# A deeper ring of early weight loads and later context loads in a three-block float32 transformer kernel

## Chip, cores and metric

The kernel runs on one core of one Trainium2 chip. The metric is the device time of one execution in microseconds. The notes below use the engines' short names: PE is TensorE (matrix products), PEld its weight loads, DVE is VectorE, ACT is ScalarE, POOL is GpSimd, and SP is the SyncE queue that issues the DMAs.

## The reference, cut to what matters

The program is a chain of three blocks on 512 tokens of width 2048, all in float32. Only the head of the first block lies near the change:

```python
sh_x, sc_x, gt_x = split(silu(c)     @ w_ada + b_ada, 3)   # w_ada: 2048 x 6144
sh_c, sc_c, gt_c = split(silu(c_ctx) @ w_ada + b_ada, 3)
h_x = rms_norm(x,   norm_g) * (1 + sc_x) + sh_x            # 512 x 2048
h_c = rms_norm(ctx, norm_g) * (1 + sc_c) + sh_c            # 256 x 2048
px = split_cols(h_x @ w_in)
pc = split_cols(h_c @ w_in)
oa, ob, oc, od = four attention mixers on px and pc
x  = x + gt_x * (concat(oa, ob, oc, od) @ w_out)
...
```

Mixer a lets every query see the 256 context keys and the 512 tokens; its first key projection is the first use of `h_c`. Two more blocks follow (a pooled block with sparse attention, and a block of sliding-window attention).

## The kernel before, in words

Every product of float32 operands is made of three matmuls on split halves: hi·hi, lo·hi and hi·lo. A weight therefore passes through three hands after its DMA: ACT writes `hi` (L569), POOL or DVE subtracts to get `lo` (L579), PE multiplies (L506 to L508 for the tokens, 512 columns wide; L511 to L513 for the context, 256 wide).

`Net.stream()` (L519) brings the weights in. They come as units of 128x512 float32 (256 KB), two units a pair, in one fixed order. The first 152 units are the start of the program: 128 units of `w_ada` and, woven between them, 24 units of the first six projections (two query heads into `px`, gates into `pc`, two halves of `S` and `O`). The modulation has four column blocks b; each is 16 units for the scale and 16 for the shift, four of them per step of PE (L682, 16 matmuls that use the raw weights as they are). After each half block PE turns the result (L656) and DVE writes `modv`. When both halves of block b stand, four k-slices of `h_x` can be made for it (`make_h`, L775): a product with the row of inverse norms (L787, DVE or POOL), the affine step and the split on ACT (L801, L303), and the low half (L306). The projections of block b run with them; the six of the last block stand at the end of the stretch. Behind them comes the first key projection of mixer a ("the first key tile" below): for each of the 16 k three matmuls on `hx` (L506 to L508) and three on `hc` (L511 to L513).

The pairs land in a ring of buffers. `ring(i)` (L530) names the pool of a pair: `wr`, `pt`, or one buffer each of two of `P`. A pair goes out as one DMA of 512 KB where its two units are neighbours in memory and in the buffer, else as two of 256 KB. SP issues in order, and a pair's DMA waits until the buffers of its pool are free; `used()` (L572) frees them when both units are done. Each DMA also waits for the one eight places ahead of it.

The context takes the same way as the tokens: `inputs()` (L719) loads it in four DMAs of 512 KB (L732, tile `xt`, source `cT`), ACT squares the 16 slices (L744), DVE or POOL adds them, PE sums over the partitions (L406), and `row()` (L383) makes the row `rc` (PE L395, ACT L398). `CMARK` (L26) says behind which pair each of the four loads may go: (40, 6) is pairs 40, 46, 52 and 58. From `rc` follow the 16 products (L787 on `xt` and `rc`), the affine steps and the splits into `hc`.

No engine's order is written by hand. A list scheduler (`Sched`, L70) runs the program's coroutines against modelled costs while the kernel is built; each operation goes to the engine's queue in the order in which the model starts it, and for `lo`, `b` and `h` it also picks DVE or POOL. So a shift of one load can give other orders on every engine behind it.

Of the kernel before, what the change touches and what calls it, by code (L numbers as in the profile page):

```python
# [16 lines left out]
DRAM = bass.MemoryType.DRAM  # L17

KT = 16
EARLY = 160  # L20
LAG = (12, 4)
WAYS = 3
EARLY_OUT = ["px", "px", "pc"]
D_ORDER = "r0 q0 h0 q1 g0 h1 g1 r1 g2 q2 h2 g3 q3 - h3"
XMARK = (4, 0.4)
CMARK = (40, 6)  # L26
EPS = 1e-6
NEG = -1e30
LOG2 = math.log(2)
# [12 lines left out]
def f32(ap):  # L42
    return ap.bitcast(F32)
# [150 lines left out]
def D2(n=0, k=1, ptr=0):  # L194

    return ("DVE", Port(D(n, k=k, ptr=ptr)[1]))
# [7 lines left out]
def A(n=0, ptr=0, acc=0, k=1):  # L204
    return ("ACT", k * (0.19 + n * 0.833e-3 + 0.093 * (ptr + acc)))


def G(n=0, k=1, bias=0.0):

    return ("POOL", Port(k * (0.15 + n * 2.2e-3)), bias)  # L210
# [13 lines left out]
class Net:  # L224
# [294 lines left out]
    def stream(self):  # L519

        ready = [Ev() for _ in self.units]
        raws = [Ev() for _ in range((len(self.units) + 1) // 2)]
        left = [min(2, len(self.units) - i) for i in range(0, len(self.units), 2)]
        nc = self.nc

        def whole(i):

            return len(self.units[i]) > 2

        def ring(i):  # L530

            return (["wr"], ["pt"], ["P", "P"], ["wr"], ["pt"], ["P", "P"])[i // 2 % 6] if i < EARLY else ["wr"]

        def wring(i):
            return ("w", "act")[i % 2] if i < EARLY else "w"

        def loads():
            for i in range(0, len(self.units), 2):
                n = min(2, len(self.units) - i)
                tags = ring(i)  # L540
                raw = yield from self.alloc(tags[0], name="wr")
                raw = [raw[:, :512], raw[:, 512:]] if len(tags) == 1 else [raw[:, :512]]
                if len(tags) > 1:
                    raw.append((yield from self.alloc(tags[1], name="wr"))[:, :512])
                src = [self.units[i + j][0] for j in range(n)]
                if n == 2 and len(tags) == 1 and src[1].offset == src[0].offset + 512:
                    both = bass.AP(tensor=raw[0].tensor, offset=raw[0].offset, ap=[raw[0].ap[0], [1, 1024]])
                    x = src[0]
                    src = [bass.AP(tensor=x.tensor, offset=x.offset, ap=[x.ap[0], [1, 1024]])]
                    dst = [both]  # L550
                else:
                    dst = raw
                for x, y in zip(dst, src):
                    yield ("SP", 0.06)
                    nc.sync.dma_start(x, y)
                self.dma_free = max(self.dma_free, self.s.now) + 1.46
                self.s.set_at(raws[i // 2], self.dma_free + 1.9, raw)
                self.s.set(self.marks.setdefault(i // 2, Ev()))

        def hi():  # L560
            for i in range(len(self.units)):
                yield raws[i // 2]
                r = raws[i // 2].val[i % 2]
                if whole(i):
                    self.s.set(ready[i], r)
                    continue
                w = yield from self.alloc(wring(i), (2, 512), F32R, "w")
                yield A(512)
                nc.scalar.activation(w[:, 0], r, AF.Copy)  # L569
                self.spawn(lo(i, w, r), 1)  # L570

        def used(i):  # L572
            left[i // 2] -= 1
            if left[i // 2] == 0:
                self.free(*ring(i))

        def lo(i, w, r):
            e = yield [D2(512), G(512, bias=WSLACK)]
            (nc.gpsimd if e == "POOL" else nc.vector).tensor_tensor(w[:, 1], r, f32(w[:, 0]), op=OP.subtract)  # L579
            used(i)  # L580
            self.s.set(ready[i], w)

        def main():
            for i, (_, fn, *_) in enumerate(self.units):
                if fn is None:
                    continue
                if whole(i):
                    for j in range(i, i + 4):
                        yield ready[j]
                    yield from fn([ready[j].val for j in range(i, i + 4)])  # L590
                    for j in range(i, i + 4):
                        used(j)
                    continue
                yield ready[i]
                w = ready[i].val
                yield from fn(w[:, 0], w[:, 1])
                self.free(wring(i))
        self.spawn(loads(), 0)
        self.spawn(hi(), 1)
        self.spawn(main(), 9)  # L600
# [633 lines left out]
    def block1(self):  # L1234
# [55 lines left out]
        def ctx():  # L1290
            rc = (yield from self.alloc("b", name="rc"))[:, :256]
            cs, cfin = self.inputs(a["cT"], 256, rc, 4, *CMARK)
            self.make_h(cs, cfin, 256, rc, 1, mods, hc, 4)
# [1098 lines left out]
```

## Time and profile before

| | |
|---|---|
| median of three runs | 2716.51 us (2716.38 to 2718.41) |
| the profiled execution | 2720.7 us, of which the span of its instructions is 2718.9 us |
| mean granted TensorE clock | 0.988 |
| busy share of the span | PE 98%, DVE 50%, ACT 44%, POOL 41% |
| chain that ended last | PE 93%, DVE 2%, DMA 2% |
| DMA | 315.97 MB, mean 116 GB/s; 355 and 328 GB/s in the first two of 40 slices of the span |

A slice is 68 us. The page's first part gives each engine's busy time; the second shows the span in 40 slices with the granted clock in tenths; the windows show the same for any stretch; the timeline lists instructions with their start, their duration and, in brackets, how long the engine stood idle before one and what released it. Start times are from the start of the span.

### The profile page before, as it was taken

Reading aid. Unit: us, or ns where it says so; the run is one execution under the profiler, and the core shown is the slowest. Engines: PE = TensorE matmul, PEld = TensorE weight load, DVE = VectorE, ACT = ScalarE, POOL = GpSimd, SP = SyncE. Lnnn points to the kernel's source line nnn. Section 1 sums busy time; section 2 is a strip of 40 time slices with the busy share of each in tenths; the row PEclk is TensorE's granted clock in tenths of the full one; section 3 lists DMA queues with packets and bytes.
Section 4 is the critical chain, followed back from the end, with each engine's and each line's share of the span. In section 5 each row is a group of like instructions: output and inputs, shape, how many; then the busy total and the mean of one; then the engine's idle time right before and its main releaser. Section 6 shows DMA issues by size and latency. Waiting matters only on the chain.

```text
span 2718.9 us, 36544 instructions
## 1 busy us (share of the span) xinstructions
PE 2655.8 (98%) x13324; PEld 2192.5 (81%) x13324; DVE 1362.8 (50%) x3151; ACT 1194.6 (44%) x2415; POOL 1121.8 (41%) x923
## 2 busy tenths in 40 slices
PE   7989999999999999899999999999999999999999
PEld 3568888888888887688887888887888888888787
DVE  3456763335552655422359466664225777676300
ACT  3444443333342445433442455554334656566421
POOL 1352333334333334344445554653444333344544
PEclk8989999999999999999999999999999999999999
DMA  9936542222221223244223322224442222222343
GB/s 355 328 102 213 182 159 69 72 72 78 70 70 64 69 67 116 78 146 145 86 78 101 109 90 89 96 87 144 147 144 90 90 93 98 84 88 86 128 142 125
DMA packets 121959, 315.97 MB, mean 116 GB/s; under 512 B 13874, under 2 KB 23986, under 8 KB 121780
## 3 DMA queue, kind: packets, MB, share of 16 engines
q1 hardware_dynamic: 121780, 313.65, 34.8%
q8 instruction: 104, 1.70, 0.3%
q14 instruction: 75, 0.61, 0.1%
HBM read 293.02 MB, written 32.11 MB: 120 GB/s over the span
## 4 chain that ended last, share of the span: by engine, by line
PE 93%; DVE 2%; DMA 2%; ACT 1%; POOL 0%; issue 0%; SPq 0%; ACTq 0%; DVEq 0%; POOLq 0%
PE px L506 23%; PE px L507 23%; PE px L508 23%; PE T L413 4%; PE S L1128 2%; PE pc L511 2%; PE pc L513 1%; PE pc L512 1%; PE T L427 1%; DMA wr<-w 1%; PE S L1825 1%; PE T L682 1%; PE S L1824 1%; PE O L1103 1%; PE O L1104 1%; PE O L1102 1%
## 5 line engine op out<-in xcount | busy, mean ns | idle before, releaser
L579 POOL TENSOR_TENSOR w<-wr,w 128x512 fp32r<-128x512 f32 x699 | 913.5, 1307 | 1418.6 <-ACT w L569 1390.2
L569 ACT ACTIVATE w<-wr 128x512 fp32r<-128x512 f32 x736 | 463.8, 631 | 1007.2 <-PE px L508 648.5
L506 PE MATMUL px<-u,w 128*128 128x512 f32 x1248 | 495.8, 397 | 0.0
L507 PE MATMUL px<-u,w 128*128 128x512 f32 x1248 | 488.3, 391 | 0.0
L508 PE MATMUL px<-u,w 128*128 128x512 f32 x1248 | 487.7, 391 | 0.0
L506 PE MATMUL px<-hx,w 128*128 128x512 f32 x816 | 330.1, 405 | 6.5 <-ACT w L569 3.5
L507 PE MATMUL px<-hx,w 128*128 128x512 f32 x816 | 323.2, 396 | 5.5 <-DVE hx L306 5.5
L508 PE MATMUL px<-hx,w 128*128 128x512 f32 x816 | 322.0, 395 | 1.8 <-POOL w L579 1.8
L506 PE MATMUL px<-o,w 128*128 128x512 f32 x752 | 297.3, 395 | 8.2 <-ACT o L303 8.2
L507 PE MATMUL px<-o,w 128*128 128x512 f32 x752 | 297.3, 395 | 3.6 <-POOL o L306 2.4
L508 PE MATMUL px<-o,w 128*128 128x512 f32 x752 | 295.9, 394 | 0.0
L508 PEld LDWEIGHTS px<-u,w 128*128 128x128 f32 x1248 | 234.7, 188 | 51.0
L506 PEld LDWEIGHTS px<-u,w 128*128 128x128 f32 x1248 | 235.4, 189 | 41.9
L507 PEld LDWEIGHTS px<-u,w 128*128 128x128 f32 x1248 | 235.3, 189 | 41.0
L306 DVE TENSOR_TENSOR pt<-T,pt 128x512 fp32r<-128x512 f32 (+2 forms) x208 | 127.7, 616 | 162.7 <-ACT pt L303 161.9
L508 PEld LDWEIGHTS px<-hx,w 128*128 128x128 f32 x816 | 154.7, 190 | 38.1 <-POOL w L579 3.2
L506 PEld LDWEIGHTS px<-hx,w 128*128 128x128 f32 x816 | 155.4, 190 | 31.3 <-ACT w L569 6.2
L507 PEld LDWEIGHTS px<-hx,w 128*128 128x128 f32 x816 | 155.3, 190 | 25.4 <-DVE hx L306 7.6
L506 PEld LDWEIGHTS px<-o,w 128*128 128x128 f32 x752 | 142.9, 190 | 39.1 <-ACT o L303 10.0
L507 PEld LDWEIGHTS px<-o,w 128*128 128x128 f32 x752 | 143.1, 190 | 37.7 <-POOL o L306 5.2
L508 PEld LDWEIGHTS px<-o,w 128*128 128x128 f32 x752 | 143.0, 190 | 29.7
L303 ACT ACTIVATE pt<-T 128x512 fp32r<-128x512 f32 (+2 forms) x208 | 110.1, 537 | 123.8 <-PE O L1104 57.3
(339 smaller groups left out, 4219.0 us busy)
## 6 DMA issues: line engine op xcount, KB each, us to landing
wr<-w SPq DMA_DIRECT2D x237, 512.0 KB, 3.5
wr<-wout SPq DMA_DIRECT2D x89, 512.0 KB, 4.1
wr<-wada SPq DMA_DIRECT2D x37, 512.0 KB, 6.5
gw<-wada SPq DMA_DIRECT2D x64, 256.0 KB, 5.7
wr<-w SPq DMA_DIRECT2D x58, 256.0 KB, 3.7
wr<-wada SPq DMA_DIRECT2D x54, 256.0 KB, 6.2
x<-xr SPq DMA_DIRECT2D x32, 256.0 KB, 4.3
xr<-x SPq DMA_DIRECT2D x32, 256.0 KB, 4.6
```

The costliest lines, as they stand in the source:

```text
L303: nc.scalar.activation(hi, src, AF.Copy)
L306: eng.tensor_tensor(lo, src, f32(hi), op=OP.subtract)
L413: self.nc.tensor.transpose(p[:, j * 128:(j + 1) * 128], x, self.ident)
L427: nc.tensor.matmul(p[:, j * gq:(j + 1) * gq], sq[:, j * 128:(j + 1) * 128], self.ones[:, 0:1] if gq == 1 else self.halves, start=True, sto ...
L506: mm(px, hi[:, s], x[0], **kw)
L507: mm(px, hi[:, s], x[1], start=False, stop=False)
L508: mm(px, lo[:, s], x[0], **ke)
L511: mm(pc, lo[:, s], c[0], **kw)
L512: mm(pc, hi[:, s], c[0], start=False, stop=False)
L569: nc.scalar.activation(w[:, 0], r, AF.Copy)
L579: (nc.gpsimd if e == "POOL" else nc.vector).tensor_tensor(w[:, 1], r, f32(w[:, 0]), op=OP.subtract)
L1128: self.nc.tensor.matmul(o, l, r, start=i == 0, stop=i == len(ops) - 1)
```

## The change

It edits two constants and the two functions that name a unit's buffers.

```diff
-EARLY = 160
+EARLY = 140, 160
...
-CMARK = (40, 6)
+CMARK = (66, 3)
...
         def ring(i):
 
-            return (["wr"], ["pt"], ["P", "P"], ["wr"], ["pt"], ["P", "P"])[i // 2 % 6] if i < EARLY else ["wr"]
+            if i < EARLY[0]:
+                return (["wr"], ["pt"], ["P", "P"], ["p", "p"], ["wr"], ["pt"], ["P", "P"])[i // 2 % 7]
+            return (["wr"], ["pt"], ["P", "P"])[i // 2 % 3] if i < EARLY[1] else ["wr"]
 
         def wring(i):
-            return ("w", "act")[i % 2] if i < EARLY else "w"
+            return ("w", "act")[i % 2] if i < EARLY[1] else "w"
```

For the first 140 units the ring is seven pairs deep instead of six: a pair in two buffers of the pool `p` comes in, which nothing else uses that early. The four context loads go behind pairs 66, 69, 72 and 75 instead of 40, 46, 52 and 58; pair 75 is the last one of the start. Lines above L531 keep their numbers; those below stand two further down. Since a pair in `P` or `p` is two buffers, the loads of `w_ada` change from 37 of 512 KB and 54 of 256 KB to 32 and 64.

The orders differ over the first 350 us or so. Three places matter here. In all of them the number behind a name tells one buffer's use from another's.

On PE, before: the row `rc` of the context is summed (T_977) in the middle of the third projection of block b = 2.

```order
L506 MATMUL pc_438<-hx_848,w_891 128x512
L507 MATMUL pc_438<-hx_848,w_891 128x512
L508 MATMUL pc_438<-hx_848,w_891 128x512
L395 MATMUL T_977<-b_961,ones 128x128 x2
L506 MATMUL pc_438<-hx_851,w_891 128x512
L507 MATMUL pc_438<-hx_851,w_891 128x512
```

On PE, now: the same sum (T_1257) stands in the last projection of block b = 3, six matmuls ahead of the first key tile (px_1283, pc_1284), whose fourth matmul reads `hc`.

```order
L508 MATMUL O_531<-hx_1098,w_1073 128x512
L395 MATMUL T_1257<-b_1208,ones 128x128 x2
L506 MATMUL O_531<-hx_1101,w_1073 128x512
L507 MATMUL O_531<-hx_1101,w_1073 128x512
L508 MATMUL O_531<-hx_1101,w_1073 128x512
L506 MATMUL O_531<-hx_1104,w_1073 128x512
L507 MATMUL O_531<-hx_1104,w_1073 128x512
L508 MATMUL O_531<-hx_1104,w_1073 128x512
L506 MATMUL px_1283<-hx_335,w_1135 128x512
L507 MATMUL px_1283<-hx_335,w_1135 128x512
L508 MATMUL px_1283<-hx_335,w_1135 128x512
L511 MATMUL pc_1284<-hc_1289,w_1135 128x256
```

So the row has moved from one projection section to the next, and nothing of `hc` can be made ahead of it.

On ACT, before: `rc` is copied out and seven slices of `hc` are done ahead of the last four slices of `hx`. These are the first rows of that stretch, and the two with which the last `hx` begins.

```order
L398 ACTIVATE rc_92<-T_977 128x256
L801 ACTIVATE b_994<-b_994,modv 128x256
L303 ACTIVATE hc_1008<-b_994 128x256
...
L801 ACTIVATE b_1149<-b_1149,modv 128x512
L303 ACTIVATE hx_1157<-b_1149 128x512
```

On ACT, now: three squares of the fourth context load (xt_1003) stand right ahead of those last slices of `hx` (the affine steps b_1087 to b_1090).

```order
L571 ACTIVATE w_1068<-wr_1000 128x512
L571 ACTIVATE w_1073<-wr_1000 128x512
L746 ACTIVATE b_1029<-xt_1003 128x256
L746 ACTIVATE b_1032<-xt_1003 128x256
L746 ACTIVATE b_1093<-xt_1003 128x256
L803 ACTIVATE b_1087<-b_1087,modv 128x512
L303 ACTIVATE hx_1095<-b_1087 128x512
```

The copy of `rc` and all 16 slices of `hc` have gone behind them, to the place after the last gate's `th`.

On POOL, now: behind the two halves w_1254 and w_1262 begin the 16 products and 16 low halves of `hc`, all on POOL (32 rows, with three L581 between them). Before, 14 of the 16 products were on DVE, and the low halves were spread from the row `rc` on.

```order
L581 TENSOR_TENSOR w_1254<-wr_1045,w_1254 128x512
L581 TENSOR_TENSOR w_1262<-wr_1045,w_1262 128x512
L789 TENSOR_TENSOR b_1278<-xt_841,rc_92 128x256
L789 TENSOR_TENSOR b_1279<-xt_841,rc_92 128x256
L306 TENSOR_TENSOR hc_1289<-b_1278,hc_1289 128x256
L306 TENSOR_TENSOR hc_1289<-b_1279,hc_1289 128x256
L789 TENSOR_TENSOR b_1299<-xt_841,rc_92 128x256
```

Products and low halves now share one queue with the weights' low halves.

## Rows read from the trace of the kernel before

**Rows 1.** The page: the span, and its first part's line on PE.

```profile
span 2718.9 us, 36544 instructions
...
PE 2655.8 (98%) x13324; PEld 2192.5 (81%) x13324; DVE 1362.8 (50%) x3151; ACT 1194.6 (44%) x2415; POOL 1121.8 (41%) x923
```

**Rows 2.** Windows of 10 us: stretch, length, busy time per engine, clock, DMA share, GB/s.

```profile
90.00:100.00 10.00, 10.00 (x53) 5.47 (x52) 1.28 (x9) 1.26 (x2) 2.57 (x2) 1.00 0.79 263
...
150.00:160.00 10.00, 8.62 (x24) 5.90 (x24) 5.83 (x9) 5.83 (x13) 7.36 (x8) 0.60 0.01 2
...
180.00:190.00 10.00, 10.00 (x55) 7.79 (x54) 6.86 (x17) 1.75 (x4) 4.26 (x5) 1.00 0.18 45
```

**Rows 3.** Timeline of PE, 70 to 140 us: start, duration, instruction, idle before.

```profile
71.03 0.95 PE L656 MATMUL T<-sel,b 128*128 128x2 f32 x8
...
79.08 0.50 PE L506 MATMUL px<-hx,w 128*128 128x512 f32 x1 [1.65 <-ACT w L569]
...
85.00 1.73 PE L682 MATMUL T<-wr,cst 128*32 128x512 f32 x8
...
113.88 0.50 PE L506 MATMUL px<-hx,w 128*128 128x512 f32 x1 [1.53 <-ACT w L569]
...
139.15 0.95 PE L656 MATMUL T<-sel,b 128*128 128x2 f32 x8
```

**Rows 4.** DMA issues: size of one, median us from issue to landing.

```profile
xt<-cT SPq DMA_DIRECT2D x4, 512.0 KB, 8.0
```

**Rows 5.** Timeline of SP, 104 to 109 us.

```profile
105.32 0.53 SPq L732 DMA_DIRECT2D xt<-cT  x1
```

**Rows 6.** Windows of 2 us around the first projections of b = 1 and b = 2.

```profile
80.00:82.00 2.00, 1.56 (x4) 1.29 (x5) 1.27 (x2) 1.14 (x4) 0.39 (x1) 0.50 1.03 395
112.00:114.00 2.00, 0.47 (x2) 0.12 (x2) 0.69 (x1) 1.55 (x4) 0.04 (x1) 1.00 1.01 370
```

**Rows 7.** Timeline of DVE, 71 to 76 us.

```profile
72.54 2.49 DVE L787 TENSOR_TENSOR b<-xt,rx 128x512 f32<-128x512 f32 x4
```

**Rows 8.** Timeline of DVE, 136 to 160 us.

```profile
140.66 6.73 DVE L787 TENSOR_TENSOR b<-xt,rx 128x512 f32<-128x512 f32 x4
```

**Rows 9.** Timeline of POOL, 126 to 170 us.

```profile
138.05 8.78 POOL L579 TENSOR_TENSOR w<-wr,w 128x512 fp32r<-128x512 f32 x6
...
163.15 1.30 POOL L579 TENSOR_TENSOR w<-wr,w 128x512 fp32r<-128x512 f32 x1 [1.29 <-issue]
```

**Rows 10.** Timeline of PE, 140 to 193 us.

```profile
143.92 0.50 PE L506 MATMUL px<-hx,w 128*128 128x512 f32 x1 [3.01 <-ACT hx L303]
148.57 0.79 PE L507 MATMUL px<-hx,w 128*128 128x512 f32 x1 [4.14 <-DVE hx L306]
...
154.53 0.80 PE L507 MATMUL px<-hx,w 128*128 128x512 f32 x1 [1.22 <-DVE hx L306]
...
158.10 0.40 PE L506 MATMUL px<-hx,w 128*128 128x512 f32 x1
...
173.84 0.39 PE L506 MATMUL px<-hx,w 128*128 128x512 f32 x1
...
175.92 0.40 PE L506 MATMUL px<-hx,w 128*128 128x512 f32 x1
...
191.88 1.04 PE L1661 MATMUL T<-b,b 33*32 33x512 f32 x2
```

**Rows 11.** Timeline of ACT, 108 to 170 us.

```profile
126.66 0.38 ACT L398 ACTIVATE rc<-T 128x256 f32<-128x256 f32 x1 [1.84 <-PE T L395]
127.54 0.60 ACT L801 ACTIVATE b<-b,modv 128x256 f32<-128x256 f32 x1 [0.49 <-DVE b L787]
128.17 0.42 ACT L303 ACTIVATE hc<-b 128x256 fp32r<-128x256 f32 x1
```

**Rows 12.** The tile `hc`, 100 to 200 us: times are min/median/max in ns, then first and last start.

```profile
L306 POOL TENSOR_TENSOR hc<-b,hc x16: 726/738/1175, 128.7 to 169.1; 128x256 fp32r<-128x256 f32 x16
```

**Rows 13.** Line 787, 120 to 170 us, in the same form.

```profile
L787 POOL TENSOR_TENSOR b<-xt,rc x2: 742/822/902, 152.2 to 165.1; 128x256 f32<-128x256 f32 x2
```

## Prediction

> **What bounds the kernel now.** I read the page first [rows 1]: PE is busy for 2655.8 of 2718.9 us. The reader should see that only some 63 us of the span are left to win, so the next question is where they lie. The windows answer it [rows 2]: from 180 us on PE is busy in all of its 10 us, while at 150 to 160 us it runs at a granted clock of 0.60 and DMA stands still. From 180 us on the program is a fixed queue of PE work, and the orders behind the first 350 us are the same before and after. So the end of the kernel moves by as much as PE's place in that queue moves, and I measure everything at one point: the end of the first key tile and of the two small matmul pairs of L1661 around it. Before, that is 191.88 + 1.04 = 192.9 us [rows 10].
>
> The timeline of PE tells what bounds the start [rows 3]. Up to 139.15 us, the last L656, PE works through the modulation as fast as `w_ada` arrives, with projection sections between in which it does not wait for DMA (263 GB/s at 90 to 100 us, [rows 2], against 395 where it does wait, [rows 6]). Behind 139.15 us the `hx` of the last block are made, PE idles up to 154.53 us, runs at half clock until 158.10, and reaches the first key tile at 173.84 [rows 10].
>
> **The change, part by part.**
>
> *The context loads leave the middle.* Four loads of 512 KB are 4 x 0.524 MB; at 395 GB/s each takes 1.33 us of the DMA [rows 4, 6]. All four stood ahead of most of the last `w_ada` loads (the last issue at 105.32 us, [rows 5]). Now the first two go between the last pairs of `w_ada`, in the stretch of the third block's projections, where DMA has slack (the 263 against 395 GB/s above), and the others behind all `w_ada`. I count three loads as gained for the last L656, since the fourth was already in such slack: 3 x 1.33 = 4.0 us.
>
> *Two more units in the ring.* While PE is in a projection section the ring fills and DMA slackens. One more pair, 0.524 MB, is 1.33 us more of loads done there. There are three such sections (b = 0, 1, 2), so this is worth between 0 and 4.0 us. I take 2.2, nearer to the middle: the start of b = 1 (79.08 to 85.00 us, [rows 3]) is also bound by its `hx` and its weight halves, which more loads don't bring. That pairs are now split into two DMAs more often costs no PE time; the queue's rate is the same for a mix of both sizes in the rows here. Together the last L656 moves by 6.2, from 139.15 to about 133.0 us. Ends: 4.0 and 8.0, and 3 if the ring gives nothing and PE's own work eats part of the rest.
>
> *The last block's `hx`.* Before, DVE began their products at 140.66 us and took 6.73 for four, 1.68 each, beside six weight halves on POOL [rows 8, 9]; alone they take 0.62 each [rows 7]. Now three squares of the fourth context load stand on ACT ahead of the affine steps. Its DMA goes out last of a burst that waits for PE to read pair 68, some 6 us ahead of the last L656, so at about 127 us; it lands 8.0 later [rows 4], at 135. That is no later than DVE's first product can be through (134.0 for `modv`, then 0.62), so it costs 0 to 1.5 us; I take 0.8. The weight halves on POOL are mostly done by then, so of the (1.68 - 0.62) x 4 = 4.2 us I take back 3.0. The last `hx` comes 6.2 - 0.8 + 3.0 = 8.4 us earlier. PE's half clock behind that pause lasts as long as before (148.57 to 158.10, [rows 10]), since the pause is much the same. The first key tile starts at 173.84 - 8.4 = 165.4 us.
>
> *What is given back: the context itself.* Before, `rc` stood at 126.66 + 0.38 = 127.0 us [rows 11] and the last low half of `hc` began at 169.1 [rows 12], ahead of the tile that reads it. Now the sum over partitions stands six matmuls ahead of the tile. Six matmuls at 0.23 are 1.4, so it runs at about 164.0, and `rc` is out at 164.5. Behind `rc` POOL has 32 passes in one queue. The nearest rows are 0.738 for a low half [rows 12] and 0.742 for a product [rows 13], both on 128x256: 32 x 0.74 = 23.7 us. Three weight halves stand between them, 3 x 1.30 = 3.9 us by the single one in POOL's rows [rows 9]. The first low half waits for one affine step and one split on ACT, 0.60 + 0.42 [rows 11], of which a second product hides most: 0.4. For passes that DVE disturbs (0.902 at most in the row of products, [rows 13]) I add 0.6. The last `hc` stands at 164.5 + 23.7 + 3.9 + 0.4 + 0.6 = 193.1, and its three matmuls end 0.5 later, at 193.6.
>
> PE alone needs (175.92 - 173.84) / 2 = 1.04 us per k [rows 10]; `hc` comes every two passes, 1.48, or 1.72 with the halves between. So PE, which has no other order than px, pc, px, pc, waits at each k, and all that it had won it spends here. Nothing covers this: the next rows of PE all stand behind the tile. Both pairs of L1661, of which one stood inside the tile before, now come behind it, since the program starts those tables only when the last `hc` stands: 193.6 + 2 x 1.04 = 195.7 us.
>
> *The sum.* 195.7 - 192.9 = +2.8 us. Against the profiled execution that gives 2720.7 + 2.8 = 2723.5; the median of the runs stands 4.2 below it (2716.5), so the forecast is **2719.3 us**. Note that a better or worse start cancels only in part: if the tile starts 1 us earlier, `rc` does too, and the end with it. With the passes at their shortest, 0.726 [rows 12], 0.4 us are won; with all of them at 0.90, 32 x 0.16 = 5.1 more are lost, so 2724.4. With a start gain of 8.0 instead of 6.2 it is 2717.5; with 4.0, 2721.5.
>
> A rule on the passes: the Trainium skill's page "SBUF — State Buffer", section "Who interferes with whom", says that a DVE instruction with two SBUF inputs and a GpSimd instruction that reads SBUF share a port pair as an exclusive lock, and the one that comes later waits. The trace agrees: four products of 0.62 alone took 1.68 each beside POOL's weight halves [rows 7 to 9]. By that rule the 32 passes lie nearer to the 0.90 end wherever DVE still runs the rope and gate steps, and the sum would be up to 2724.4; I keep the short price because DVE has given the products of `hc` away and so has less to collide with.
>
> **The rivals.**
>
> *Slower, by the clock.* In the tile PE now waits up to 0.7 us at every k. If the granted clock falls to 0.5 there, a k costs twice its 1.04, 2.08 us, more than the 1.72 at which `hc` comes, and PE is the bound: 165.4 + 16 x 2.08 = 198.7 instead of 193.6. Up to 5.1 more, 2724.4; half of it, with recovery inside the tile, gives 2721.9; the full one with a half clock of some 9 us behind it (as at 148.57 to 158.10, [rows 10]), which loses half of that on top, 2729. I price it at 2724.4. For it: at 80 to 82 us the clock was 0.50 after PE had waited for loads and halves; against it: at 112 to 114 us PE was busy for 0.47 of 2 us and stayed at 1.00 [rows 6]. It decides if the waits come at every k as they do here. The Trainium skill's page "TensorE: Matmul & The Clock Gate", section "HAM oscillation — how this bites in real kernels", describes that: a kernel whose PE waits inside each tile falls back to the slow clock in every tile. Chance 0.17.
>
> *Slower, by the loads.* The start gains only 3 us: the eight DMAs in flight, not the buffers, limit the run-ahead, and more halves than full pairs fill those eight places. Then all moves 3.2 later: 2722.5. For it: more DMAs of 256 KB are issued. Against it: three context loads are gone from the middle in any case. Chance 0.16.
>
> *Faster.* `hc` does not bind: the tile starts at 165.4 and runs through at 1.04 per k, and the kernel wins the 8.4 us, 2708.1. It would need two passes of POOL in 1.04 us, or products that go out ahead of the low halves and ACT. Against it: 0.726 is the shortest pass in the rows [rows 12]. A half-way case (the start wins 10 us or more and the tile loses less) gives 2710. Chance 0.12.
>
> **How the numbers follow.** The forecast has 0.55, the two slower rivals 0.33, the faster one 0.12. This kernel's measurement can tell about 0.2%, 5.4 us, from no change: faster is below 2711.1, slower above 2721.9. The forecast case reaches from 2715 to 2724 by its bounds (start gain, pass time); I give 0.50 of it to no change and 0.05 to slower. The slower rivals are both priced above the line. So: faster 0.12, same 0.50, slower 0.38. For 8 in 10 I leave out the faster rival's lower half and the clock's worst case: 2711.5 to 2727.0.
>
> **What the new profile would show.** Right: the last L656 at 131 to 135 us; the first matmul of the first key tile at 164 to 167; `rc` (now L398 behind the last `th`) at about 164.5; 32 passes on POOL from there to about 193, with PE's L512 waiting for POOL's `hc` at most k; L1661 twice behind the tile; 1.00 in the clock at 165 to 195. The first rival shows as a clock of 0.5 there, the second as a last L656 at 136 or later. The forecast is wrong if PE's idle time inside the tile sums to less than 5 us, or if the queue of PE behind 200 us shows waits that the old one did not have.

## Result and profile after

The change made the kernel slower: 2733.72 us (median of four runs, 2731.72 to 2735.34) against 2716.95 us (four runs, 2716.38 to 2718.41). The ratio is 1.0054, 95% interval 1.0039 to 1.0068. The forecast was 2719.3 us in a range of 2711.5 to 2727.0; the time lies above it. The profiled executions stand 2733.04 to 2720.7 us, 12.3 apart; the one of before lay 3.75 us above the median of its runs, the one of after 0.7 below. All medians leave out the only execution in a slow state, 8738.10 us in the run e8.

The page of the changed kernel, against [rows 1]: the span has grown by 12.0 us, and PE's busy time has not.

```profile
span 2730.9 us, 36536 instructions
## 1 busy us (share of the span) xinstructions
PE 2654.2 (97%) x13324; PEld 2194.2 (80%) x13324; DVE 1349.9 (49%) x3130; ACT 1199.5 (44%) x2422; POOL 1126.9 (41%) x937
```

So PE stands idle for 76.7 us instead of 63.1. The windows of 10 us say where, against [rows 2], whose row for 180 to 190 us had PE busy for all of it.

```profile
140.00:150.00 10.00, 3.82 (x16) 2.59 (x16) 6.18 (x13) 6.17 (x11) 6.50 (x6) 0.82 0.94 341
...
170.00:180.00 10.00, 8.27 (x36) 6.12 (x34) 3.21 (x7) 6.26 (x14) 8.30 (x11) 0.85 0.16 52
180.00:190.00 10.00, 7.08 (x31) 5.70 (x32) 0.00 (x0) 5.45 (x13) 10.00 (x14) 0.84 0.00 0
190.00:200.00 10.00, 8.77 (x46) 7.13 (x46) 3.55 (x2) 7.52 (x16) 10.00 (x14) 0.96 0.10 28
```

From 180 to 200 us POOL is busy without a gap and PE is not: the first key tile waits for the context, as forecast. But the tile should have begun at 165.4 us. The timeline of PE, against [rows 3, 10], shows when things came.

```profile
25.17 1.92 PE L684 MATMUL T<-wr,cst 128*32 128x512 f32 x4 [10.93 <-DMA wr<-wada]
...
32.71 1.87 PE L658 MATMUL T<-sel,b 128*128 128x2 f32 x8
...
84.96 0.51 PE L506 MATMUL px<-hx,w 128*128 128x512 f32 x1 [1.82 <-ACT hx L303]
86.34 0.50 PE L507 MATMUL px<-hx,w 128*128 128x512 f32 x1 [0.88 <-DVE hx L306]
...
140.28 0.95 PE L658 MATMUL T<-sel,b 128*128 128x2 f32 x8
148.12 0.79 PE L506 MATMUL px<-hx,w 128*128 128x512 f32 x1 [6.07 <-ACT hx L303]
...
173.29 0.39 PE L506 MATMUL px<-hx,w 128*128 128x512 f32 x1
...
199.52 0.39 PE L513 MATMUL pc<-hc,w 128*128 128x256 f32 x1 [1.17 <-POOL hc L306]
...
200.67 0.28 PE L513 MATMUL pc<-hc,w 128*128 128x256 f32 x1
```

The last L658 (L656 before) comes at 140.28 instead of 139.15 us, where 133.0 was forecast; the tile begins at 173.29 instead of 173.84; and it ends at 200.67 + 0.28 = 200.95 us instead of 191.95. It held one pair of L1661 before and holds none now, so PE stands 9.0 + 1.04 = 10.0 us further back. Of the other 2 us, 1.4 are small waits behind it: in the five stretches of 25 us from 200 to 325 us PE lacks 0.94, 0.68, 0, 0.33 and 0 us, where it lacked 0.28, 0, 0, 0 and 0.30 before.

Three other timelines of the changed kernel belong to this. SP, where the fourth context load goes out, and ACT, where the context's squares and `rc` stand (against [rows 11]):

```profile
137.34 0.37 SPq L734 DMA_DIRECT2D xt<-cT  x1
```

```profile
143.93 1.03 ACT L746 ACTIVATE b<-xt 128x256 f32<-128x256 f32 x3 [0.70 <-DMA xt<-cT]
146.59 0.81 ACT L803 ACTIVATE b<-b,modv 128x512 f32<-128x512 f32 x1 [1.62 <-DVE b L789]
...
172.11 0.39 ACT L398 ACTIVATE rc<-T 128x256 f32<-128x256 f32 x1
```

And DVE, against [rows 8], with the add of those squares ahead of the products for `hx`:

```profile
141.26 0.60 DVE L664 TENSOR_SCALAR modv<-T,vec 128x2 f32<-128x2 f32 x4 [2.26 <-PE T L658]
144.38 0.50 DVE L751 TENSOR_TENSOR b<-b,b 128x256 f32<-128x256 f32 x1 [2.52 <-ACT b L746]
144.80 3.55 DVE L789 TENSOR_TENSOR b<-xt,rx 128x512 f32<-128x512 f32 x4
```

The passes for `hc` in the view of tiles and lines, against [rows 12, 13]: 32 on POOL, at 0.73 each.

```profile
L306 POOL TENSOR_TENSOR hc<-b,hc x16: 717/729/744, 175.4 to 199.4; 128x256 fp32r<-128x256 f32 x16
...
L789 POOL TENSOR_TENSOR b<-xt,rc x16: 718/732/747, 173.5 to 196.8; 128x256 f32<-128x256 f32 x16
```

### The profile page after: what moved, and what is told of

Read it like the earlier page. It is cut to its first block, busy times and chain, and to the rows that moved or that the text cites. A ratio compares the mean times of both kernels' runs of the same rounds, so it can differ in the third digit from the quotient of the medians.

```text
span 2730.9 us, 36536 instructions
## 1 busy us (share of the span) xinstructions
PE 2654.2 (97%) x13324; PEld 2194.2 (80%) x13324; DVE 1349.9 (49%) x3130; ACT 1199.5 (44%) x2422; POOL 1126.9 (41%) x937
## 4 chain that ended last, share of the span: by engine, by line
PE 91%; DVE 2%; DMA 2%; POOL 1%; ACT 1%; issue 1%; SPq 0%; DVEq 0%; ACTq 0%; POOLq 0%
PE px L506 23%; PE px L507 23%; PE px L508 23%; PE T L413 4%; PE S L1130 2%; PE pc L511 1%; PE pc L513 1%; PE pc L512 1%; PE T L427 1%; PE T L684 1%; PE S L1827 1%; PE S L1826 1%; PE O L1105 1%; PE O L1106 1%; PE O L1104 1%
## 5 line engine op out<-in xcount | busy, mean ns | idle before, releaser
L581 POOL TENSOR_TENSOR w<-wr,w 128x512 fp32r<-128x512 f32 x700 | 912.5, 1304 | 1463.2 <-ACT w L571 1444.3
```

## The experiments

Four theories came out of this; the first two began as one, called Q in the first expectations (the context's queue behind `rc`). **L**: `rc` is late, since the fourth context load is the last load of the start, and the tile waits for all that follows `rc`. **P**: the queue on POOL is the cost, wherever `rc` stands. **S**: the ring costs the start, because the eight token loads now go out in one block ahead of the eighth pair. **O**: the order on ACT costs the first projections of blocks b = 1 and 2. Each run is compared with the kernel before, run on the same chip. Differences between two runs are those of their medians; e1 to e4 ran on one chip and e5 to e12 on another, and with each taken against its own runs of the kernel before, such a difference comes out up to 2 us otherwise (16.1 instead of 16.75 for e9 and e3, 17.4 instead of 16.7 for e10 and e4, 5.9 instead of 5.25 for e11 and e4, 8.25 instead of 6.6 for the changed kernel and e5). A trace shows one execution: that of e2 lay 4.3 us above the median of its runs, that of e12 5.5 below.

### The parts alone

e1 undoes the second part of the change (`-CMARK = (66, 3)`, `+CMARK = (40, 6)`) and keeps the ring.

> The deeper ring alone, with the context loads at the old pairs (40, 6). Theory Q (the loss is the context's queue: rc comes six matmuls ahead of the first key tile and 32 passes on POOL follow it): rc is early again, about 127 us, no wait for hc in the tile, and the time is near the old one, 2713 to 2720 us. Theory S (the ring itself costs: all eight token loads now go out ahead of the eighth pair, the first L658 comes at 32.7 instead of 24.0 us, PE stays at half clock to 41 us): the first projection still comes at 49 to 50 us, and the time is 2718 to 2722 us. Theory R (the loads split into 256 KB halves carry the loss everywhere): 2728 us or more.

Measured: 2711.31 us, ratio 0.9973 (0.9961 to 0.9985). The ring alone is faster than the kernel before, and a little more than Q's range had it, so R falls. S holds in the main for the first 50 us (L658 at 33.02, first projection at 48.66 where 49 to 50 was said), but the end was better than it said: the last L658 comes at 136.82 and the tile is not stalled.

e2 is the other half: the kernel before with `CMARK = (66, 3)`.

> The later context loads alone, on the old ring. Theory Q: rc stands six matmuls ahead of the tile as in the changed kernel, so the tile waits for hc; but here all products but one are on DVE, so POOL has 17 passes (some 12.5 us and three weight halves, 4 us) instead of 32: the tile loses 3 to 8 us where the changed kernel lost some 10, and the time is 2719 to 2726 us. Theory S: without the ring the start is the old one (first L656 at 24 us), the context loads out of the way win 3 to 4 us, and the time is 2712 to 2717 us.

Measured: 2722.06 us, ratio 1.0013 (1.0003 to 1.0023). Q's bounds hold and S's don't. The last L656 came at 138.35 us, 0.8 earlier than before: the context loads out of the way had won almost nothing. The two ratios multiply to 0.9986, where the change measured 1.0054; the parts are bad together.

### The token loads

e3 is e1 with `-XMARK = (4, 0.4)`, `+XMARK = (5, 0.4)`; e4 is the changed kernel with the same edit. Why: in the kernel before SP sent five token loads, a pair of weights, and then three; in the changed one all eight in a row. The timelines of SP, first before, then after:

```profile
5.25 4.23 SPq L732 DMA_DIRECT2D xt<-xT  x5
...
13.13 1.60 SPq L555 DMA_DIRECT2D wr<-wada  x2
15.64 2.92 SPq L732 DMA_DIRECT2D xt<-xT  x3
```

```profile
7.14 6.35 SPq L734 DMA_DIRECT2D xt<-xT  x8
```

> The deeper ring with the old context loads, and the token loads marked behind pair 5 instead of 4 (XMARK), so that they go out five and three again, with a pair of weights between. Theory S: first L658 at 25 to 27 us, first projection at 46 to 48 us, 2 to 3 us faster than the ring alone: 2711 to 2717 us. If S is not it, the time is that of the ring alone within 1 us.

Measured: 2708.30 us, ratio 0.9961 (0.9946 to 0.9976), below the range expected; its first L658 is back at 24.40 us and its last at 132.46, 6.7 ahead of the kernel before.

> The changed kernel with the token loads marked behind pair 5. Theory S: 2 to 3 us faster than the changed kernel, 2730 to 2732 us, since the start is mended and the rest is not. Theory Q with an unlimited part in S: the time is that of the changed kernel, 2733 to 2734 us, if PE's later waits on hx of the last block (bound by the fourth context load) take the gain up.

Measured: 2731.55 us, ratio 1.0042 (1.0027 to 1.0057); the last L658 at 137.38. So S is small, 2 to 3 us in both versions. By the times alone it is not clear of the noise, since the ranges of each pair of runs overlap; the traces show it, with the last L658 4.4 us earlier in e3 than in e1 and 2.9 earlier in e4 than in the changed kernel.

### The late row

e9 is the fast version e3 with a single load moved: the fourth context load.

```diff
                 mark = first + int(k // per * every)
+                if per == 4 and k == 12:
+                    mark = 75
```

> The fast version (deeper ring, token loads behind pair 5, context loads at pairs 40, 46, 52) with the fourth context load alone moved behind pair 75. Theory L (the late rc is the cause, and rc waits for the last of the four loads alone): rc comes at 163 to 170 us, the tile waits for hc, the hx of the last block wait for the squares of that load; 2722 to 2730 us, 14 to 20 more than with the load at pair 58. Theory M (it takes all four loads late, through the DMA or ACT's order in the blocks before): less than 2716 us.

Measured: 2725.05 us, ratio 1.0024 (1.0014 to 1.0035), 16.75 more than e3. e3 and e4 differ in the context loads alone and stand 23.25 us apart; that one load carries 16.75 of it. PE and ACT of e9:

```profile
131.53 0.95 PE L658 MATMUL T<-sel,b 128*128 128x2 f32 x8
139.98 0.79 PE L506 MATMUL px<-hx,w 128*128 128x512 f32 x1 [6.00 <-ACT hx L303]
...
167.27 0.39 PE L511 MATMUL pc<-hc,w 128*128 128x256 f32 x1 [1.24 <-ACT hc L303]
...
179.78 0.58 PE L513 MATMUL pc<-hc,w 128*128 128x256 f32 x1 [2.73 <-POOL hc L306]
...
191.42 0.39 PE L513 MATMUL pc<-hc,w 128*128 128x256 f32 x1 [1.17 <-POOL hc L306]
```

```profile
L398 ACT ACTIVATE rc<-T x1: 385/385/385, 164.0 to 164.0; 128x256 f32<-128x256 f32 x1
```

Modulation as early as in e3, the last `hx` held back as in the changed kernel, and from `rc` on the same waits.

e10 goes the other way: the kernel of e4 with `-CMARK = (66, 3)`, `+CMARK = (57, 3)`.

> The changed kernel with the token loads behind pair 5 and the context loads nine pairs earlier: 57, 60, 63, 66 instead of 66, 69, 72, 75. Theory L: rc stands at about 130 us, the tile does not wait for hc, the last hx are not held by squares; the time falls by at least 12 us, to 2710 to 2719 us (the upper end if the planner's order again lets the last L658 wait for ACT, as it did with 54, 58, 62, 66). Theory P (POOL's queue wherever rc stands): 2724 us or more.

Measured: 2714.84 us, ratio 0.9983 (0.9973 to 0.9993), 16.7 less than e4. `rc` stands at 131.3 us and no matmul of the tile waits. Both directions give the same size; L stands. The expected accident came too: PE waits 6.35 us for the last L658, because five slices of `hc` stand on ACT in front of the copy that it needs.

```profile
142.94 1.87 PE L658 MATMUL T<-sel,b 128*128 128x2 f32 x8 [6.35 <-ACT b L318]
```

e5 and e6 ask what POOL's queue costs by itself. e5 is the changed kernel with all products for `hc` on DVE; e6 is e3 with products and low halves of `hc` all on POOL.

```diff
-            e = yield [D2(n), G(n)]
+            e = yield [D2(n), G(n)] if n == 512 else [D2(n)]
```

```diff
-            e = yield [D2(n), G(n)]
+            e = yield [D2(n), G(n)] if n == 512 else [G(n)]
...
-            yield from self.split(hi, lo, u, pool=True)
+            yield from self.split(hi, lo, u, pool=True if n == 512 else 2)
...
-            e = yield ([D2(n), G(n, bias=SLACK)] if pool else D(n))
+            e = yield ([G(n)] if pool == 2 else [D2(n), G(n, bias=SLACK)] if pool else D(n))
```

> The changed kernel with all 16 products for hc on DVE, so that POOL has 16 passes behind rc instead of 32. Theory P (POOL's queue is what costs): 16 passes x 0.73 = 11.7 us less on POOL, of which DVE's 0.42 to 1.0 each gives some back; the tile ends 6 to 10 us earlier and the time is 2724 to 2728 us. Theory L (the late rc costs, whichever engine makes the products, since the first hc cannot stand before 174 us and DVE and POOL hold each other up): 2 to 5 us earlier, 2729 to 2732 us.

Measured: 2727.13 us, ratio 1.0031 (1.0019 to 1.0043): 6.6 less than the changed kernel, a time within P's bounds and beyond L's. The trace stands between the two: its last wait for `hc` is at 195.96 us behind an `rc` at 173.6; in the changed kernel 199.52 behind 172.1, so 5 us less from `rc` on, but only 3.6 earlier, where P had 6 to 10 and L 2 to 5.

> The best run so far (deeper ring, token loads behind pair 5, context loads at the old pairs), with all products and all low halves of hc forced on POOL: 32 passes in one queue, but behind an early rc at about 123 us. Theory L: the queue has 40 us until the first key tile and is nearly hidden, 2708 to 2712 us. Theory P: 32 passes hold up the weight halves and the tile wherever rc stands, 2715 us or more.

Measured: 2706.44 us, ratio 0.9955 (0.9940 to 0.9970). The same 32 passes on POOL behind an `rc` at 123.6 us cost nothing:

```profile
L306 POOL TENSOR_TENSOR hc<-b,hc x16: 723/750/1189, 126.1 to 163.2; 128x256 fp32r<-128x256 f32 x16
```

So P is not a theory of its own: the queue's length counts, and only behind a late `rc`.

e7 is e3 with `-CMARK = (40, 6)`, `+CMARK = (54, 4)`.

> The deeper ring, token loads behind pair 5, and the context loads halfway, behind pairs 54, 58, 62 and 66; the sum for rc then stands at the end of the second block's projections, some 8 us later than in the run with the old pairs, and still 50 us ahead of the tile. Theory L: no wait in the tile; if the context loads in the middle cost the modulation anything, the last L658 comes up to 4 us earlier, 2704 to 2708 us. If moving them gives the start nothing, as in the run with the marks alone, or costs it, because ACT's order changes, 2708 to 2713 us.

Measured: 2717.74 us, ratio 0.9997 (0.9987 to 1.0006). Both guesses missed. `rc` at 131.5 us did no harm, but the last L658 waited 4.45 us for ACT's copy, the accident of e10, and stands at 140.48. e12 puts the loads earlier than before (e3 with `+CMARK = (34, 6)`).

> The deeper ring with the token loads behind pair 5 and the context loads six pairs earlier than before (34, 40, 46, 52). If an early rc is all that counts, nothing is left to win there: 2706 to 2711 us, the same as with 40, 46, 52, 58. If context loads cost the start wherever they stand ahead of a wait for DMA, the last L658 moves by up to 1.3 us either way, 2707 to 2710 us. More than 2714 us would mean that the order on ACT matters more than the loads.

Measured: 2717.05 us, ratio 0.9993 (0.9983 to 1.0002), 8.7 more than e3, though `rc` comes at 117.6 and the last L658 at 134.26. Here PE waits 3.56 us at 143.47 for a low half of `hx` on DVE. That the order which falls out of the shift costs more than the shift itself fits this, but no run tests it alone, and the traced execution, 2711.50 us, shows only a part of the 8.7.

### The order on ACT

Why did the context loads, once gone, not free the start? In e4 PE waits for an `hx` in the first projection of b = 1:

```profile
81.45 0.49 PE L506 MATMUL px<-hx,w 128*128 128x512 f32 x1 [1.51 <-ACT hx L303]
...
137.38 0.95 PE L658 MATMUL T<-sel,b 128*128 128x2 f32 x8
```

ACT has this stretch there. The second projection's weights (second row) are split ahead of the last `hx` (third row):

```profile
78.33 0.80 ACT L803 ACTIVATE b<-b,modv 128x512 f32<-128x512 f32 x1
80.25 0.63 ACT L571 ACTIVATE w<-wr 128x512 fp32r<-128x512 f32 x1 [1.12 <-DMA wr<-w]
80.79 0.61 ACT L303 ACTIVATE hx<-b 128x512 fp32r<-128x512 f32 x1
```

ACT waits for a DMA with the `hx` behind it, for which PE waits. With the context loads in the middle, as in e3, the planner reckoned with a later landing and put that `hx` first. e8 tells the planner that all pairs land 2 us later (`self.dma_free + (3.9 if i < EARLY[0] else 1.9)`).

> The changed kernel with the token loads behind pair 5, and the planner told that a pair lands 2 us later (3.9 behind the port instead of 1.9) for the first 140 units; nothing else is edited. Theory O (ACT's order: a weight split is planned ahead of the last hx split and waits on the chip for its DMA, so hx is late and PE waits 1.5 to 1.8 us and falls to half clock in the first projections of b = 1 and 2): hx comes first, the waits on hx at 81 and 115 us go, the last L658 comes 2 to 5 us earlier than 137.4 us, and the time is 2726 to 2730 us. If ACT's order is not it, the last L658 stays at 136 to 138 us and the time at 2730 to 2733 us.

Measured: 2735.72 us, median of five (four at 2735.06 to 2736.47, one at 2727.12; what parts them was not looked into, and the trace is of one of the four), ratio 1.0055 (1.0041 to 1.0069). The time is outside O's range. The waits on `hx` went, as O said, but the first projection's weights were now planned late too, and PE waited for those (2.52 us at 81.71, 1.90 at 115.25); the last L658 came at 140.48. The edit moved more than it should test, so e11 pins the one split behind the one `hx`:

```diff
+                if i in self.behind:
+                    yield self.behind[i]
...
+        self.behind = {at[id(first[1][b])]: split[4 * b + 3] for b in (1, 2)}
```

(`split[k]` is set when the `hi` half of slice k is planned; the lines that set it move the line numbers in the rows below by up to four.)

> The changed kernel with the token loads behind pair 5, and in the blocks b = 1 and 2 the split of the second projection's weights pinned behind the last hx split on ACT; nothing else changes place there. Theory O (ACT's order behind a late DMA costs the first projections): PE's waits on hx at 81 and 115 us (1.5 and 1.3 us, with 0.9 on the low half behind each) shrink below 0.6, the last L658 comes at 132 to 134 us instead of 137.4, and the time is 2726 to 2728 us. If DMA alone sets these sections, the last L658 stays at 136 to 138 us and the time at 2730 to 2733 us.

Measured: 2726.30 us, ratio 1.0037 (1.0027 to 1.0047), 5.25 less than e4. ACT and PE of e11:

```profile
78.30 0.63 ACT L303 ACTIVATE hx<-b 128x512 fp32r<-128x512 f32 x1
79.45 0.63 ACT L575 ACTIVATE w<-wr 128x512 fp32r<-128x512 f32 x1 [0.51 <-DMA wr<-w]
```

```profile
79.71 0.50 PE L509 MATMUL px<-hx,w 128*128 128x512 f32 x1 [0.23 <-DVE hx L308]
...
130.86 0.95 PE L662 MATMUL T<-sel,b 128*128 128x2 f32 x8
```

The last L658 (L662 there) comes 6.5 us earlier than in e4. Of this 0.9 stood already at the L658 of 71 us, ahead of the exchange; the other 5.7 come from two exchanged rows on ACT, twice, and from what the planner moved with them: in each of the two blocks one copy of `T` went from ACT to DVE, which the expectation had excluded. PE's wait of 1.51 us on `hx` is gone, and O is shown by the traces; the times point the same way, but the intervals of e4 and e11 overlap.

## Why the prediction was wrong, step by step

The time missed the forecast by 14.4 us. Of these, 9.2 lie between the spans (12.0 us more instead of 2.8), and the steps below account for them. Most of the rest is the step from a trace to the runs: the forecast took 4.2 us off, since the traced execution of before lay that far above its runs, but the one of after lay 0.7 below its own.

**PE's queue behind the tile is fixed: right.** Taken from the end of the tile with the pairs of L1661 allowed for, the rest is the same within 2 us: 2718.9 - 192.9 = 2526.0 before, 2730.9 - 200.95 - 2.1 = 2527.9 after. Still, a sign that the forecast had named for being wrong came: waits behind 200 us that the old queue did not have, the 1.4 us above.

**The last L656 moves by 6.2 us to 133.0: this step failed.** It came at 140.28. The four versions split the way there: the ring, with the orders that came with it, won 6.7 (139.15 to 132.46, e3), the context loads out of the way 1.6 (to 130.86, e11), the order on ACT cost 6.5 (to 137.38, e4; 5.7 without what stood ahead of the exchange), the token loads in one block 2.9 (to 140.28). By terms: the ring was put at 2.2, too low, though no run parts its buffers from the orders; the context loads at 4.0, where 1.6 is hardly more than the scatter of this point, since two kernels with the same orders up to there (the changed one and e5) have it at 140.28 and 141.70. The order on ACT and that of SP's token loads were not in the sum at all. Both stood in the two programs' orders; I had looked there for the context's instructions alone, and had costed a transfer out of the way without asking what the planner would put in its place.

**The last `hx`.** The fourth context load was to go out 6 us ahead of the last L656, to land at 135 us and to cost 0.8; it went out 2.9 us ahead (137.34), ACT waited for it to 143.93, and DVE's first product, behind the add of its squares, came 2.9 us after `modv` (144.80 against 141.26 + 0.60). The products then took 0.89 each instead of 1.68, 3.2 us in all, where 3.0 was put. From the last L658 to the tile it took 33.0 us instead of 34.7, so 1.7 less where 2.2 was put. All in all the tile's start moved by 0.55 us, not 8.4, and nearly all of the difference is the start's.

**The price of the context: right in its sum.** (Two rows stand behind this point.) From the end of `rc` to the end of the tile the sum had 193.6 - 164.5 = 29.1 us; measured 200.95 - 172.5 = 28.45. The 32 passes took 0.73 each, and three weight halves stood between. The way through the tile was another: PE waited at six places, 5.9 us in all, and not at each k, since POOL ran up to three products or three low halves in a row. e9 is the forecast's own case: its `rc` came out at 164.4 where 164.5 was put, and its span is 2722.8 us, 3.9 above that of before, where the sum had 2.8 (by the medians of the runs it is 6.2). The passes did not come near their 0.90 end, since DVE stood idle beside them for 20.91 us (the first row below, of the changed kernel). Where products were on DVE, as in e2 (the second row), they took 0.95 us in the median instead of the 0.42 that they need alone, beside POOL's low halves. Both agree with the rule of the Trainium skill's page "SBUF — State Buffer", section "Who interferes with whom", which the prediction tells.

```profile
196.44 0.69 DVE L947 SCALAR_TENSOR_TENSOR th<-th,O 128x512 f32<-128x512 f32 x1 [20.91 <-ACT th L945]
```

```profile
L787 DVE TENSOR_TENSOR b<-xt,rc x15: 410/948/1512, 175.6 to 189.9; 128x256 f32<-128x256 f32 x15
```

**The rivals.** *By the clock:* the granted clock did fall in the tile, twice (0.85 and 0.84 in the windows above; 0.50 in the row below, of the changed kernel, behind a wait of 2.73 us), but the tile's end did not come later by it: behind both falls PE still waits 1.17 us for POOL at 199.52, and POOL is busy without a gap from 180 to 200 us. POOL set the pace. The fall agrees with the Trainium skill's page "TensorE: Matmul & The Clock Gate", section "HAM oscillation — how this bites in real kernels", which tells of a kernel whose PE waits inside each tile and falls back to the slow clock there. *By the loads:* its sign came, a last L656 behind 136 us, but not because the buffers could not be used; e1 and e3 use them and win. *Faster:* `hc` not binding is e3, with the context loads left where they were.

```profile
188.00:190.00 2.00, 2.00 (x7) 1.71 (x8) 0.00 (x0) 0.07 (x1) 2.00 (x4) 0.50 0.00 0
```

**What stays open.** The 2 us of waits behind the tile were not traced to their cause. Why the kernel before ran at 2718.2 to 2718.8 us in the later comparisons and at 2716.95 in the first was not looked into; each ratio is against its own runs.

Four of the runs beat both kernels by more than their intervals: e1, e10, and, fastest, e3 at 2708.30 us and e6 at 2706.44, whose ranges overlap (2707.03 to 2710.60 and 2703.43 to 2709.89). e1, e3 and e6 are the deeper ring without the later context loads.

## To carry to other kernels

When a planner orders in-order queues, a transfer taken out of the way is not won time: read on every engine what now stands ahead of the work that the bound engine waits for, and which of it waits for a DMA. A load that many small passes hang on must be timed from its last user backwards: here one transfer of 1.33 us sat ahead of 28 us of work, and 17 pairs' difference in its place was worth some 16 us. And test the parts of a change alone, since a good part can hide behind a bad one.

## What was not expected

A clock at half speed in the very tile that waits was without price, since another engine set the pace. And a block of loads in another order in the first 20 us cost its 2.9 us in two ways. The first is the clock: PE stood still for 10.93 us, and then had half the clock until about 40 us, where the kernel before had it back by 35 (the windows of before and after follow). With that the second L658 came at 41.12 us, where e4 has it at 39.93.

```profile
30.00:35.00 5.00, 5.00 (x28) 1.66 (x22) 2.10 (x10) 0.30 (x1) 0.00 (x0) 0.82 1.03 403
35.00:40.00 5.00, 4.76 (x29) 2.25 (x28) 0.68 (x4) 1.20 (x2) 0.00 (x0) 1.00 1.03 400
```

```profile
30.00:35.00 5.00, 5.00 (x28) 2.50 (x24) 1.74 (x10) 0.00 (x0) 0.00 (x0) 0.50 1.03 398
35.00:40.00 5.00, 5.00 (x24) 1.99 (x16) 0.74 (x6) 0.60 (x1) 0.00 (x0) 0.50 1.04 399
```

In both DMA ran at 398 to 403 GB/s in these stretches. The second way is ACT again: before, the split of the first projection's weights stands ahead of the fourth `hx`, as it does in e4, and in the changed kernel behind it.

```profile
46.17 0.63 ACT L569 ACTIVATE w<-wr 128x512 fp32r<-128x512 f32 x1 [0.48 <-DMA wr<-w]
...
47.54 0.63 ACT L303 ACTIVATE hx<-b 128x512 fp32r<-128x512 f32 x1
```

```profile
48.39 0.63 ACT L303 ACTIVATE hx<-b 128x512 fp32r<-128x512 f32 x1
48.93 0.61 ACT L571 ACTIVATE w<-wr 128x512 fp32r<-128x512 f32 x1
```

```profile
49.60 0.50 PE L506 MATMUL px<-hx,w 128*128 128x512 f32 x1 [3.35 <-ACT w L571]
```

PE's first projection waited 3.35 us for that split, against 0.29 before. This is read from the rows and was not tested alone.
